# A list schedule extended through branch, output and gate/up stages, and the first two weight blocks on ACT's queue

## Chip, core and metric

The kernel runs on one core of one Trainium2 chip. The metric is the device time of one execution in microseconds (us). The engines are TensorE (PE), VectorE (DVE), ScalarE (ACT), GpSimd (POOL) and SyncE (SP); DMAs are issued from the queue of SP or of ACT.

## What is computed

A decoder block on x of 1024 tokens by 1024 channels, in float32: two mixers side by side, merged by gates, and a SwiGLU feed-forward part.

```python
xn = rms_norm(x, norm1_g)
q_sb, k_sb, v_sb, q_hg, f_hg, i_hg, g_hg, gate_sb, gate_hg = split_cols(xn @ w_in)
o_sb = stick_breaking_attention(rms(q), rms(k), v)         # 8 heads of 64
o_hg = hgrn2_mixer(q_hg, f_hg, i_hg, g_hg, lb, hg_norm_g)  # 4 heads of 128
y_sb = o_sb @ w_branch[:512]
y_hg = o_hg @ w_branch[512:]
mixed = sigmoid(gate_sb) * y_sb + sigmoid(gate_hg) * y_hg
h = x + mixed @ w_out
hn = rms_norm(h, norm2_g)
out = h + (silu(hn @ w_gate) * (hn @ w_up)) @ w_down       # 2816 hidden channels
```

## The kernel before

Channels lie on the partitions, tokens along the free axis in two halves of 512. Each float32 operand of a large product is split in two float32r parts, hi (a cast) and lo (the difference, on DVE), and a product of 128 x 128 weights with 128 x 512 data is three matmuls, hi hi, hi lo and lo hi (`mm3`, `prod`). Every such matmul is a 128x512 one. The stages follow each other:

1. S1, the stage of the mixers: x is loaded, its squares summed, xn split; 42 column blocks of `w_in` are projected (`proj`), 16 of them the gates (called G; their results go to DRAM, `sig_d`), and the heads of the two mixers run (`scores`, `values`, `hgrn`; outputs to DRAM, `o_d`). All of it is written as operations of a `Plan`: each has an engine, an estimated duration, a rank, and the buffers it needs from rings with a fixed number of slots. `Plan.issue` (L124 to L199) runs a simulated clock, and whenever an engine is free it issues the first ready operation in the order of rank and then of `way`, the longest chain of estimated durations to the end. The order found so is the instruction order of each engine (`manual_schedule`). Projections have rank -1, so PE turns to them when nothing else is ready; what remains of the G projections comes last.
2. wb, the branch products (L783 to L821): o_d is loaded and split, then for eight column blocks the gates are loaded, multiplied by the row scale `rr1` on POOL (L808), put through a sigmoid on ACT, multiplied with the products and added.
3. wo, the output projection with the residual (L834 to L890): h is stored to `h_d`, and the right operands of the next stage, `fop[1..7]`, are built from sums of its blocks (Winograd's variant of Strassen's product: seven products of half-size blocks in place of eight).
4. Gate and up (L898 to L1024): for each of 11 pairs of hidden blocks, `left` loads two weight blocks and builds seven split left operands (`a_ops`), `winograd` runs seven products of 12 matmuls for gate, and then for up. `down_sums` builds sums of the down weights for the last stage and stores them to `wd_d`; the activations and their sums go to `act_d`. The products' banks are x, y and z; y is read (`c[:, 1]`, L981; `c[:, 3]`, L986) before the next product is added into it.
5. Down (L1027 to L1102), seven products over the 11 pairs, with the residual.

Stages 2 to 5 are written in plain order and are ordered by the framework's own scheduler, which may put their instructions between those of the planned stage too. Line 182 of the profile is the one that issues every planned operation of S1. L237 and L238 are the casts and differences of `split`.

In the start, SP issues in turn the constants `vec`, x's blocks and four weight half blocks: x0, wq (first half of block q), x1, wk, x2, x3, wq (second half), x4, wk. POOL casts these weights (`split_w`). ACT's first instruction is the load of an activation table (L205). Nine dummy matmuls (L341) precede the first product.

Of the kernel before, what the change touches and what calls it, by code (L numbers as in the profile page):

```python
# [66 lines left out]
class Buf(View):  # L67
    def __init__(self, ring, make):
        super().__init__(self, lambda t: t)
        self.ring, self.make, self.tile = ring, make, None  # L70
        self.writers, self.readers, self.left, self.held = [], [], 0, False


class Plan:
# [6 lines left out]

    FROM = {"P": 0.2, "D": 2.0}
    TO = {"P": 0.35}

    def __init__(self):
        self.ops, self.caps, self.land = [], {}, {}

# [3 lines left out]
    def op(self, eng, us, calls, rank=0, after=(), part=False, holds=(), lat=None, land=None):  # L91
# [27 lines left out]
        self.ops.append((eng, us, calls, rank, deps, after, bufs, lat))  # L119
        if land:  # L120
            self.land[i] = land
        return i

    def issue(self):  # L124
# [18 lines left out]

        way = [0.0] * n
# [6 lines left out]
        early = [0.0] * n  # L151
# [6 lines left out]
        times, gone, done, t = [0.0], [], 0, 0.0  # L158
        while done < n:
# [6 lines left out]
            for e in engines:  # L166
                while free[e] <= t:
                    for i in ready[e]:
                        need = [b for b in ops[i][6] if b.ring and not b.held]
                        if early[i] <= t and all(  # L170
                                slots[b.ring] >= sum(c.ring == b.ring for c in need)
                                for b in need):
                            break
                    else:
                        break
                    ready[e].remove(i)
                    _, us, calls, rank, deps, after, bufs, lat = ops[i]
# [25 lines left out]
def hybrid_block(ctx: ExitStack, tc, xT, wi, wb, wo, wg, wu, wd, vec, outT):  # L203
    nc = tc.nc
    nc.scalar.preload_act_table_set("natural_log_exp_and_others")  # L205

# [89 lines left out]

    def hs(h):
        return slice(h * HALF, (h + 1) * HALF)
# [25 lines left out]
    xn = a_set(xst.enter_context(tc.tile_pool(name="xnp", bufs=1)))  # L324
    pre = ExitStack()
# [22 lines left out]
    st1 = ExitStack()  # L348
    tmpp = st1.enter_context(tc.tile_pool(name="tmpp", bufs=1, reuse_waits="tile"))
    stk = st1.enter_context(tc.tile_pool(name="stk", bufs=1, reuse_waits="tile"))  # L350
    att = st1.enter_context(tc.tile_pool(name="att", bufs=1, reuse_waits="tile"))
    hgp = st1.enter_context(tc.tile_pool(name="hgp", bufs=1, reuse_waits="tile"))
# [9 lines left out]
    where = {tag: (pool, cap) for pool, tags in RINGS.items() for tag, cap in tags.items()}  # L362

    def new(tag, shape=(P, HALF), dt=F32):
        pool, cap = where[tag]
        plan.ring(tag, cap)
        return Buf(tag, lambda: pool.tile(list(shape), dt, tag=tag, bufs=cap, name=tag))
# [4 lines left out]
    def A(fn, *args, n=HALF, aps=0, rank=0, ps=False, part=False, holds=(), **kw):  # L372
        us = (0.05 if ps else 0.093) + n / 1200 + 0.0935 * aps
        return plan.op("A", us, [(fn, args, kw)], rank, part=part, holds=holds)
# [23 lines left out]

    act, tt = nc.scalar.activation, nc.vector.tensor_tensor
    stt, ts = nc.vector.scalar_tensor_tensor, nc.vector.tensor_scalar  # L400

    def rstd(dst, ss, n, rank=0):
        A(act, dst, ss, AF.Ln, ps=True, aps=1, bias=eps_t, scale=1.0 / n, rank=rank)
        A(act, dst, dst, AF.Exp, scale=-0.5, rank=rank)
# [35 lines left out]
    def load(dst, src, kb):  # L440
        last_load[0] = L(dst, src, kb, rank=1, after=(last_load[0],))
# [12 lines left out]
    def take_x(h):  # L454
        ss, acc, ws, sqs = new("ms"), new("tail"), [[], []], []
        for k in range(KT):
            x = new("aa" if h == 0 else ("xf", "xq", "xi", "xg")[k // 2])
            load(x, xT[k][:, hs(h)], 256)
            if h == 0 and k in (0, 1, 3, 4):
                u, i = k % 3, k // 3  # L460
                n, v = fill[u]
                w = new("kb")
                load(w, wi[COL[n] + v][:, hs(i)], 256)
# [59 lines left out]
    def take(nm, u, h, ps):  # L523
# [17 lines left out]
        elif nm == "G":  # L541
            x = new("tmp")
            A(nc.scalar.copy, x, ps, ps=True)
            plan.op("A", 0.1, [(nc.scalar.dma_start, (sig_d[u][:, hs(h)], x), {})], lat=2.5)
# [19 lines left out]

    COL = {"q": 0, "k": 4, "v": 8, "hq": 12, "hf": 16, "hi": 20, "hg": 24, "G": 28}
# [34 lines left out]
    def values(j, last):  # L600
# [12 lines left out]
        for e in range(2):  # L613
            own, oth = slice(64 * e, 64 * e + 64), slice(64 - 64 * e, 128 - 64 * e)
            for sb in range(4):
# [29 lines left out]
                L(o_d[j][own, sb * 256:(sb + 1) * 256], ot[own], 64)  # L645
        return last

    def hgrn(hd, last):
# [5 lines left out]
        for h in range(2):  # L654
# [89 lines left out]
            L(o_d[4 + hd][:, hs(h)], o, 256)  # L744
# [3 lines left out]
    fill = [("q", 0), ("k", 0), ("v", 0), ("hf", 0), ("hq", 0), ("hi", 0)]  # L748
# [11 lines left out]
    for i, (nm, u) in enumerate(fill):  # L760
# [7 lines left out]
        elif i > 1:  # L768
            w = take_w(COL[nm] + u)
# [6 lines left out]
            if nm == "hg":  # L776
                ends = [f(u, e) for f, e in zip((scores, values, hgrn), ends)]
    with tc.manual_schedule():
        plan.issue()
    c1.close()  # L780
    st1.close()
    st2 = ExitStack()
    op_ = st2.enter_context(tc.tile_pool(name="opool", bufs=1, side="right", reuse_waits="tile"))  # L783
    mt = st2.enter_context(tc.tile_pool(name="mt", bufs=2, side="right", reuse_waits="tile"))
    oo = []
    for k in range(KT):
        t = mt.tile([P, S], F32, tag="ld", bufs=4, name="o32")
        nc.sync.dma_start(t, o_d[k])
        hi = op_.tile([P, S], F32R, name=f"oh{k}")
        lo = op_.tile([P, S], F32R, name=f"ol{k}")  # L790
        nc.scalar.copy(hi, t)
        nc.vector.tensor_tensor(lo, t, hi.bitcast(F32), op=ALU.subtract)
        oo.append((hi, lo))
    xst.close()
    mst = ExitStack()
    mx = a_set(mst.enter_context(tc.tile_pool(name="mxp", bufs=1, reuse_waits="tile")))
    wq = [get_w(wb[0])]
    for i in range(KT):
        w = wq.pop(0)
        if i + 1 < KT:  # L800
            wq.append(get_w(wb[i + 1]))
        s0 = mt.tile([P, S], F32, tag="s0", bufs=2, name="s0")
        s1 = mt.tile([P, S], F32, tag="s1", bufs=2, name="s1")
        nc.sync.dma_start(s0, sig_d[i])
        nc.sync.dma_start(s1, sig_d[KT + i])
        for s in (s0, s1):
            for h in range(2):
                nc.gpsimd.tensor_tensor(s[:, hs(h)], s[:, hs(h)], rr1[h], op=ALU.mult)  # L808
            nc.scalar.activation(s, s, AF.Sigmoid)
        for h in range(2):  # L810
            y0, y1 = pj(), pz()
            mm3(y0, w, full[:4], oo, h)
            mm3(y1, w, full[4:], oo, h)
            t0 = mt.tile([P, HALF], F32, tag="t0", name="t0")
            t1 = mt.tile([P, HALF], F32, tag="t1", name="t1")
            nc.vector.tensor_tensor(t0, y0, s0[:, hs(h)], op=ALU.mult)
            nc.vector.tensor_tensor(t1, y1, s1[:, hs(h)], op=ALU.mult)
            nc.vector.tensor_tensor(t0, t0, t1, op=ALU.add)
            nc.scalar.copy(mx[i][0][:, hs(h)], t0)
            nc.vector.tensor_tensor(mx[i][1][:, hs(h)], t0, mx[i][0][:, hs(h)].bitcast(F32),  # L820
                                    op=ALU.subtract)  # L821
    st2.close()
    rst.close()

    fst = ExitStack()
    s2p = fst.enter_context(tc.tile_pool(name="s2p", bufs=2, side="right", reuse_waits="tile"))
    fpool = fst.enter_context(tc.tile_pool(name="fpool", bufs=1, side="right", reuse_waits="tile"))
    fop = {p: [None] * 4 for p in ORDER}
    rr = [fpool.tile([P, HALF], F32, name=f"rr{h}") for h in range(2)]

    def ft(dt, name):
# [319 lines left out]
```

## Time and profile before

| | us |
|---|---|
| median of three runs (lowest, highest) | 1529.68 (1528.2, 1530.11) |
| the profiled execution's own time | 1531.17 |
| its span, first to last instruction | 1529.4 |
| PE busy | 1500.8 (98%) |
| DVE busy | 1179.9 (77%) |
| ACT busy | 799.1 (52%) |
| POOL busy | 160.5 (10%) |

The span is that of one profiled execution. Matmuls overlap each other in the array, so a busy PE counts a pipeline that holds at least one of them; a 128x512 matmul is shown with some 0.39 us and the next one starts 0.227 us later. The granted clock is given as a share of TensorE's full 2.4 GHz. A row of the windows view has start:end, the length, then for PE, PEld (PE's weight loads), DVE, ACT and POOL the busy us and (x) the number of instructions, and at the end the granted clock, the share of the DMA engines' time and GB/s.

### The profile page before, as it was taken

The numbers are of one execution on the slowest core, as the hardware profiler recorded it, in microseconds if no ns is written. First come the engines' busy times: TensorE is split into PE (matmuls) and PEld (weight loads), VectorE is DVE, ScalarE is ACT, GpSimd is POOL, SyncE is SP. The second block draws the span as 40 slices with busy tenths as digits, with TensorE's granted clock in tenths as the row PEclk, the third lists the DMA queues.
The fourth block names the chain that finished last, engine by engine and source line by source line (L and its number), as shares of the span: only waits on it lengthen the run. The fifth ranks groups of instructions, "written<-read, shape, count | busy, mean of one in ns | idle before, by whom it ended". The sixth has DMA issues, their size and how long they took to land.

```text
span 1529.4 us, 20448 instructions
## 1 busy us (share of the span) xinstructions
PE 1500.8 (98%) x7213; PEld 1241.2 (81%) x7213; DVE 1179.9 (77%) x2060; ACT 799.1 (52%) x1503; POOL 160.5 (10%) x189
## 2 busy tenths in 40 slices
PE   8999999999999999999999979999999999999999
PEld 6788888888888888888878868888888888878887
DVE  8899779987898777965557789888887777475553
ACT  7866768578858879444333352333333333254442
POOL 4210111111111110114420000000000000000000
PEclk9999999999999999999999999999999999999999
DMA  5111211111111121145434436666633333687672
GB/s 180 42 39 42 83 32 43 47 44 59 41 51 54 59 68 49 52 143 208 139 111 150 140 128 223 221 214 220 221 110 110 111 110 117 245 302 223 191 220 93
DMA packets 78407, 188.53 MB, mean 123 GB/s; under 512 B 9056, under 2 KB 11104, under 8 KB 76896
## 3 DMA queue, kind: packets, MB, share of 16 engines
q1 hardware_dynamic: 68368, 168.34, 33.7%
q10 hardware_dynamic: 9936, 18.88, 3.3%
q8 instruction: 57, 0.93, 0.3%
q14 instruction: 46, 0.38, 0.1%
HBM read 131.61 MB, written 55.57 MB: 122 GB/s over the span
## 4 chain that ended last, share of the span: by engine, by line
PE 72%; DVE 12%; DMA 6%; ACT 4%; issue 4%; POOL 2%; SPq 0%; POOLq 0%; ACTq 0%; DVEq 0%
PE pj L182 24%; PE f L919 20%; PE f L1068 12%; PE ms L182 8%; PE z L182 2%; DMA w<-wu 2%; PE pj L306 2%; PE pj L305 2%; PE pj L307 2%; DVE ol L238 2%; DMA s<-sig_d 1%; ACT aa L182 1%; DMA rb<-act_d 1%; POOL s L808 1%; DMA h_d<-xx 1%
## 5 line engine op out<-in xcount | busy, mean ns | idle before, releaser
L182 PE MATMUL pj<-ah,oh 128*128 128x512 f32 x704 | 286.6, 407 | 1.9 <-POOL oh L182 1.9
L182 PE MATMUL pj<-ah,ol 128*128 128x512 f32 x704 | 276.4, 393 | 1.1 <-DVE ol L182 1.0
L182 PE MATMUL pj<-al,oh 128*128 128x512 f32 x704 | 276.0, 392 | 0.0
L919 PE MATMUL f<-fh,oh 128*128 128x512 f32 x616 | 241.4, 392 | 11.2 <-ACT p L970 7.1
L919 PE MATMUL f<-fl,oh 128*128 128x512 f32 x616 | 240.5, 390 | 0.0
L919 PE MATMUL f<-fh,ol 128*128 128x512 f32 x616 | 240.4, 390 | 0.0
L237 ACT CAST oh<-w 128x512 fp32r<-128x512 f32 x168 | 102.5, 620 | 186.6 <-PE f L919 132.2
L182 PEld LDWEIGHTS pj<-ah,ol 128*128 128x128 f32 x704 | 132.6, 188 | 31.8 <-DVE ol L182 2.4
L182 PEld LDWEIGHTS pj<-ah,oh 128*128 128x128 f32 x704 | 133.0, 189 | 25.4 <-POOL oh L182 2.9
L182 PEld LDWEIGHTS pj<-al,oh 128*128 128x128 f32 x704 | 133.0, 189 | 22.7 <-issue 0.5
L919 PEld LDWEIGHTS f<-fh,oh 128*128 128x128 f32 x616 | 116.1, 189 | 38.4 <-ACT p L970 7.6
L238 DVE TENSOR_TENSOR ol<-w,oh 128x512 fp32r<-128x512 f32 x168 | 115.1, 690 | 35.5 <-ACT oh L237 35.2
L919 PEld LDWEIGHTS f<-fh,ol 128*128 128x128 f32 x616 | 116.1, 188 | 24.5
L919 PEld LDWEIGHTS f<-fl,oh 128*128 128x128 f32 x616 | 116.2, 189 | 23.8
L182 DVE TENSOR_TENSOR_SCAN aa<-aa,ww 128x128 f32<-128x128 f32 (+3 forms) x96 | 92.2, 975 | 33.4 <-ACT aa L182 23.9
L1068 PE MATMUL f<-bh,ah 128*128 128x512 f32 x296 | 114.9, 390 | 1.1 <-ACT acc L1094 1.1
L1068 PE MATMUL f<-bl,ah 128*128 128x512 f32 x296 | 115.4, 390 | 0.5 <-DVE bl L238 0.5
L1068 PE MATMUL f<-bh,al 128*128 128x512 f32 x296 | 115.2, 389 | 0.0
L182 POOL TENSOR_SCALAR oh<-w 128x512 fp32r<-128x512 f32 x84 | 71.1, 846 | 394.2 <-PE pj L182 355.2
L238 DVE TENSOR_TENSOR al<-ra,ah 128x512 fp32r<-128x512 f32 x73 | 50.4, 690 | 76.8 <-ACT ah L237 76.8
L237 ACT CAST ah<-ra 128x512 fp32r<-128x512 f32 x73 | 45.6, 625 | 104.0 <-PE f L1068 92.9
L182 ACT ACTIVATE aa<-aa 128x512 f32<-128x512 f32 (+3 forms) x128 | 69.1, 553 | 4.9 <-DVE aa L182 4.0
(270 smaller groups left out, 2971.2 us busy)
## 6 DMA issues: line engine op xcount, KB each, us to landing
w<-wi SPq DMA_DIRECT2D x42, 512.0 KB, 3.6
rb<-act_d SPq DMA_DIRECT2D x73, 256.0 KB, 4.4
w<-wg SPq DMA_DIRECT2D x22, 512.0 KB, 4.1
w<-wu SPq DMA_DIRECT2D x22, 512.0 KB, 3.7
w<-wd SPq DMA_DIRECT2D x22, 512.0 KB, 7.0
wd_d<-ds SPq DMA_DIRECT2D x44, 256.0 KB, 5.6
ra<-wd_d SPq DMA_DIRECT2D x44, 256.0 KB, 4.1
act_d<-c SPq DMA_DIRECT2D x10, 1024.0 KB, 3.9
```

The costliest lines, as they stand in the source:

```text
L182: fn(*[a.real() if isinstance(a, View) else a for a in args], **{k: v.real() if isinstance(v, View) else v for k, v in kw.items()})
L237: pin(nc.scalar.copy(hi, src))
L238: pin(nc.vector.tensor_tensor(lo, src, hi.bitcast(F32), op=ALU.subtract))
L305: nc.tensor.matmul(out, hi[:, ws], a[ka][0][:, hs(h)], start=first and i == 0, stop=False)
L306: nc.tensor.matmul(out, hi[:, ws], a[ka][1][:, hs(h)], start=False, stop=False)
L307: nc.tensor.matmul(out, lo[:, ws], a[ka][0][:, hs(h)], start=False, stop=last and i == n - 1)
L808: nc.gpsimd.tensor_tensor(s[:, hs(h)], s[:, hs(h)], rr1[h], op=ALU.mult)
L919: nc.tensor.matmul(out, a[i][:, ws], bl[k][j], start=start and k == 0 and i + j == 0, stop=k == 3 and i == 1, skip_group_check=True)
L1068: nc.tensor.matmul(bank[d], l[:, ws], r, start=start and i == 0, stop=p == NP - 1 and i == 2, skip_group_check=True)
```

## The change

- **The plan takes in wb, wo and gate/up.** Every operation gets a part (`s1`, `G`, `wb`, `wo`, `ffn`). Those of the later parts come after all ready ones of S1 and G on their engine (`STAGE`), and `way` counts only inside S1 and G or inside the later parts. New tile pools open when every operation of the parts named in `BEFORE` has been issued.
- **New in these stages:** the multiplications of the gates by `rr` go to DVE; temporaries of wo come from the ring `f` of 56 slots, and `t7` and `t6` overwrite `blk` tiles; `g` and `c` are four tiles of 512 columns each and are stored as four DMAs, not one; the first gate product group is ordered 1, 5, half of 2, 6, channel sums, 7, half of 2, 4, 3; PSUM banks come from the rings pj (x), ms (y) and z (z) of S1.
- **The start:** ACT issues the first halves of the blocks q and k before its table load, and casts them itself; SP's order is `vec`, x0, x1, x2, wq (second half), x3, wk (second half), x4 to x7.

Down is unchanged, but its pool of PSUM banks opens after the planned part. The core of the diff:

```diff
+    STAGE = {"s1": 0, "G": 0, "wb": 1, "wo": 1, "ffn": 1}
+    BEFORE = {0: (), 2: ("s1",), 3: ("s1", "G"), 4: ("s1", "G", "wb"), 5: ("s1", "G", "wb", "wo")}
...
-                [way[j] + delay(i, j, data) for j, data in succ[i] if ops[j][3] >= 0 or data],
-                default=0.0)
-        order = lambda i: (-ops[i][3], -way[i], i)
+                [way[j] + delay(i, j, data) for j, data in succ[i]
+                 if stage[i] == stage[j] and (ops[j][3] >= 0 or data)], default=0.0)
+        order = lambda i: (stage[i], -ops[i][3], -way[i], i)
...
-    nc.scalar.preload_act_table_set("natural_log_exp_and_others")
...
+    for n, v in fill_cols[:2]:
+        t = hgp.tile([P, HALF], F32, tag="kb", bufs=4, name="kb")
+        nc.scalar.dma_start(t, wi[COL[n] + v][:, :HALF])
+        first_w.append(t)
+    nc.scalar.preload_act_table_set("natural_log_exp_and_others")
...
+            for u in range(2):
+                w = Buf("kb", lambda u=u: first_w[u])
+                hi, lo = new("oh", dt=F32R), new("ol", dt=F32R)
+                plan.at[A(nc.scalar.copy, hi, w, rank=3)] = 2.4 + 0.6 * u
+                V(tt, lo, w, hi.bitcast(F32), op=ALU.subtract, rank=2)
+                ws[u].append((hi, lo))
...
-            if h == 0 and k in (0, 1, 3, 4):
-                u, i = k % 3, k // 3
+            if h == 0 and k in (2, 3):
+                u = k - 2
...
+    mx = []
+    for i in range(KT):
+        w = get_w(wb[i])
...
+            for h in range(2):
+                V(tt, t[:, hs(h)], t[:, hs(h)], rr[h], op=ALU.mult)
+            A(act, t, t, AF.Sigmoid, n=S + (0 if i or ss else TABLE))
...
+                    t7, t6 = blk[0, 1], blk[0, 0]
+                    V(tt, t7, y, t7, op=ALU.subtract)
+                    V(tt, t6, t7, t6, op=ALU.add)
...
+    def winograd(a, ring, first=False):
+
+        c = [new(ring) for _ in range(4)]
+        x, y, z, p1 = new("pj"), new("ms"), new("z"), new("p1")
+        prod(x, a, 1, True)
+        A(nc.scalar.copy, p1, x, ps=True)
+        if first:
+            prod(z, a, 5, True)
+            prod(x, a, 2, False, (0, 1))
+            prod(y, a, 6, True)
+            channel_sums()
+            V(tt, c[1], y, p1, op=ALU.add)
+            prod(y, a, 7, False)
+            prod(x, a, 2, False, (2, 3))
...
+    for p in range(NP):
+        au = left(wu, p, "wA")
+        x, g = winograd(ag, "g", p == 0)
...
+        for b, t in enumerate((*c, n7, n6, n5, n4)):
+            dst = actd[p][:, b * HALF:(b + 1) * HALF]
+            store_a(dst, t) if p == NP - 1 else L(dst, t, 256, part=True)
+
     with tc.manual_schedule():
         plan.issue()
-    c1.close()
-    st1.close()
```

## Rows read from the trace of the kernel before

**Rows 1.** windows by stage: start:end, then length, busy us of engines, clock, DMA

```profile
21.21:702.10 680.89, 674.65 (x3620) 564.29 (x3620) 566.27 (x1074) 487.74 (x984) 113.24 (x141) 1.00 0.19 61
702.10:790.80 88.70, 87.29 (x385) 71.95 (x384) 51.90 (x73) 32.42 (x45) 38.22 (x28) 1.00 0.36 123
790.80:877.86 87.06, 87.06 (x385) 72.07 (x384) 62.59 (x105) 32.05 (x56) 0.00 (x0) 1.00 0.43 138
877.86:1313.23 435.37, 424.19 (x1854) 348.49 (x1852) 361.58 (x582) 144.67 (x239) 0.00 (x0) 0.99 0.47 160
```

**Rows 2.** windows over single gate/up pairs of 168 matmuls

```profile
936.89:976.13 39.24, 38.42 (x169) 31.46 (x169) 34.67 (x57) 11.93 (x20) 0.00 (x0) 1.00 0.62 215
...
1053.95:1092.73 38.78, 38.38 (x168) 31.45 (x168) 34.57 (x57) 12.00 (x21) 0.00 (x0) 1.00 0.64 217
1092.73:1130.83 38.10, 38.09 (x168) 31.52 (x169) 32.24 (x52) 12.55 (x22) 0.00 (x0) 1.00 0.51 164
```

**Rows 3.** waits of PE, whole kernel: total us, times, longest

```profile
PE f L919 <- ACT p L970: 7.1, 1, 7.1
PE f L919 <- DVE g L981: 3.0, 5, 0.8
...
PE z L305 <- DVE t L817: 1.4, 1, 1.4
```

**Rows 4.** timeline of PE from wo into gate: start, us, instruction, idle before

```profile
885.12 0.39 PE L919 MATMUL f<-fh,ol 128*128 128x512 f32 x1
892.64 0.79 PE L919 MATMUL f<-fh,oh 128*128 128x512 f32 x1 [7.14 <-ACT p L970]
...
897.08 0.42 PE L919 MATMUL f<-fl,oh 128*128 128x512 f32 x1
...
898.24 1.09 PE L932 MATMUL f<-parts,ones_r 128*128 128x512 f32 x4
...
905.34 0.50 PE L919 MATMUL f<-fh,oh 128*128 128x512 f32 x1 [0.99 <-DVE g L986]
```

**Rows 5.** timelines of ACT and DVE, same stretch

```profile
892.01 0.58 ACT L970 COPY p<-f 128x512 f32<-128x512 f32 x1
...
885.43 0.69 DVE L884 TENSOR_TENSOR t<-yy 128x512 f32<-128x512 f32 x1 [2.89 <-DMA h_d<-xx]
```

**Rows 6.** chain that ended last, and waits of SP's queue, 905 to 1095

```profile
957.49 5.71 DMA w<-wu
...
SPq L958 <- DVE ds L945: 79.6, 16, 10.8
```

**Rows 7.** groups by line: count, busy us and mean ns, idle before

```profile
L808 POOL TENSOR_TENSOR s<-s,rr 128x512 f32<-128x512 f32 x32 | 43.3, 1380 | 59.5 <-DMA s<-sig_d 59.5
```

**Rows 8.** timeline of PE in the start

```profile
5.68 0.74 PE L182 MATMUL pj<-ah,oh 128*128 128x512 f32 x1
...
9.17 0.50 PE L182 MATMUL pj<-ah,oh 128*128 128x512 f32 x1 [1.85 <-POOL oh L182]
...
20.94 0.39 PE L182 MATMUL pj<-ah,ol 128*128 128x512 f32 x1
```

**Rows 9.** timelines of SP, ACT and POOL in the start

```profile
1.24 0.41 SPq L182 DMA_DIRECT2D aa<-xT  x1
...
0.80 1.28 ACT L205 ACT_TABLE_LOAD   x1 [0.80 <-PEq L1133]
...
8.05 1.07 POOL L182 TENSOR_SCALAR oh<-kb 128x512 fp32r<-128x512 f32 x1 [2.42 <-DMA kb<-wi]
```

**Rows 10.** windows of the start

```profile
1.24:4.27 3.03, 2.83 (x7) 2.25 (x8) 1.78 (x15) 1.14 (x3) 2.48 (x4) 1.00 0.67 180
4.27:7.13 2.86, 2.73 (x7) 1.22 (x5) 1.82 (x3) 1.24 (x2) 0.62 (x1) 1.00 0.86 216
...
9.17:17.00 7.83, 7.54 (x26) 5.68 (x26) 7.83 (x12) 7.83 (x15) 4.24 (x8) 0.78 1.05 393
```

**Rows 11.** windows of 25 us, second one

```profile
25.00:50.00 25.00, 22.70 (x94) 17.07 (x93) 23.28 (x38) 16.47 (x28) 15.09 (x21) 1.00 0.15 43
```

More of the change, by code (lines that the diff above doesn't have):

```diff
@@ L169, in issue @@
                         need = [b for b in ops[i][6] if b.ring and not b.held]
-                        if early[i] <= t and all(
+                        if early[i] <= t and not any(
+                                left[p] for p in self.BEFORE[phase[i]]) and all(
                                 slots[b.ring] >= sum(c.ring == b.ring for c in need)
@@ L369, in fixed, with new, make, A @@
+    def new(ring, shape=(P, HALF), dt=F32):
+        pool, cap, tag, phase = where[ring]
+        plan.ring(ring, cap)
+        def make():
+            open_pools(phase)
+            return (pools[pool] if phase else pool).tile(list(shape), dt, tag=tag, bufs=cap, name=tag)
+        return Buf(ring, make, phase)
     def fixed(tile):
         return Buf(None, lambda: tile)
-    def A(fn, *args, n=HALF, aps=0, rank=0, ps=False, part=False, holds=(), **kw):
+    def A(fn, *args, n=HALF, aps=0, rank=0, ps=False, part=False, holds=(), after=(), **kw):
@@ L776, in hybrid_block, with full_split, get_w @@
             if nm == "hg":
+                plan.part = "s1"
                 ends = [f(u, e) for f, e in zip((scores, values, hgrn), ends)]
+    def full_split(src, rings=("oh", "ol"), rank=0):
+        hi, lo = new(rings[0], dt=F32R), new(rings[1], dt=F32R)
+        A(nc.scalar.copy, hi, src, rank=rank)
+        V(tt, lo, src, hi.bitcast(F32), op=ALU.subtract, rank=rank)
+        return hi, lo
+    def get_w(src):
+        t = new("w", (P, 1024))
+        load(t, src, 512, rank=0)
+        return [full_split(t[:, 512 * i:512 * i + 512]) for i in range(2)]
@@ new lines, in hybrid_block, with products @@
+    TABLE = 1536
+    plan.part = "wb"
+    turn = last_fill[0]
+    oo = []
+    for k in range(KT):
+        t = new("ld", (P, S))
+        L(t, od[k], 512)
+        hi, lo = new("oo", (P, S), F32R), new("oo", (P, S), F32R)
+        A(nc.scalar.copy, hi, t, n=S)
+        V(tt, lo, t, hi.bitcast(F32), op=ALU.subtract, n=S)
+        oo.append((hi, lo))
+    def products(out, w, a, ks, h, k0=0, last=True):
+        nonlocal turn
+        for n, k in enumerate(ks):
+            hi, lo = w[(k0 + n) // 4]
+            ws = slice((k0 + n) % 4 * P, ((k0 + n) % 4 + 1) * P)
+            turn = M(1536, [(out, hi[:, ws], a[k][0][:, hs(h)], n == 0, False),
+                            (out, hi[:, ws], a[k][1][:, hs(h)], False, False),
+                            (out, lo[:, ws], a[k][0][:, hs(h)], False, last and n == len(ks) - 1)],
+                     after=(turn,))
@@ new lines, in hybrid_block, with left @@
+    last_wu, last_wd = [None], [None]
+    def left(src, p, ring):
+        A_ = "A" if ring == "wA" else ""
+        sp = lambda t: full_split(t, ("oh" + A_, "ol" + A_))
+        ta, tb = new(ring, (P, 1024)), new(ring, (P, 1024))
+        for t, r in ((ta, src[p]), (tb, src[p + NP])):
+            if A_:
+                last_wu[0] = L(t, r, 512, after=(last_wu[0],))
+            else:
+                load(t, r, 512, rank=0)
+        a11, a12, a21, a22 = ta[:, :512], ta[:, 512:], tb[:, :512], tb[:, 512:]
+        s2 = new("s2")
+        ops = {1: sp(a11)}
+        V(tt, a21, a11, a21, op=ALU.subtract)
+        V(tt, s2, a22, a21, op=ALU.subtract)
+        ops[6] = sp(s2)
+        V(tt, a11, s2, a11, op=ALU.add)
+        ops[5] = sp(a11)
+        ops[7] = sp(a21)
+        ops[2] = sp(a12)
+        ops[4] = sp(a22)
+        V(tt, a12, a12, s2, op=ALU.subtract)
+        ops[3] = sp(a12)
+        return ops
```

447 lines of the change are left out of this document (206 added, 241 removed).

## The prediction

> **What bounds the kernel now.** I read the profile stage by stage first: one row of the windows view for each stage [rows 1]. TensorE (PE) is busy in 674.65 of the 680.89 us of the first stage (the hand-written list schedule, S1 below), 87.29 of 88.70 in the branch stage (wb), all 87.06 of the output projection (wo), and 424.19 of 435.37 in gate and up. So PE is the bound throughout, and only what PE doesn't do can be won: idle time, time at the lower clock, and late starts inside "busy". For the floor of a stage I take its own best stretch. Wo, with the same 384 matmuls as wb, took 87.06 us, 0.227 us each: wb loses 88.70 - 87.06 = 1.64. One gate/up pair of 168 matmuls ran without a gap in 38.10 us [rows 2]; eleven make 419.1, and the four channel-sum matmuls [rows 4] at 0.227 each 0.9. Gate/up loses 435.37 - 420.0 = 15.3 us. That is the largest loss with one address, and the list schedule is extended over exactly that stage.
>
> Next, who ended PE's waits [rows 3]: one wait of 7.1 us in gate/up for ACT's copy `p1` (L970), five of at most 0.8 for DVE's L981, one of 1.4 in wb (bank z, L305).
>
> **Gate/up, part by part.** Its first product group ends near 885.35; PE starts again at 892.64 [rows 4]: 7.3 us. When it starts, ten matmuls need 897.08 - 892.64 = 4.44 us instead of 2.27: the granted clock was at its lower level, 1.2 GHz, after that idle stretch, another 2.2 us. Why was ACT's copy so late? It ran at 892.01, behind casts of the weight splits and of `fh`, which wait for DVE; DVE itself stood 2.89 us at 885.43 because `t7` (L884) takes a slot whose old content, `xx`, was still being stored to h_d [rows 5]. The change removes both: `t7` becomes `blk[0, 1]` in place, `xx` comes from the ring of 56, and `p1` goes onto ACT by its rank on the path, not behind splits that aren't due. All of 7.3 + 2.2 can go. What takes its place is DVE: after the last wo matmul it owes some 10 instructions of the last block, 6 of gate's weight splits, 2 channel sums, 5 evacuations and 8 of up's splits before the 20 us of the first winograd are over: 31 at 0.62 us (32.24 us for 52, [rows 2]) = 19 us. It fits with nothing to spare, so I leave 2.5 us of stalls here. Bounds: 0, and the 9.5 us of before.
>
> The pairs from 936.89 on: four stretches last 39.24 to 38.78 rather than 38.10 [rows 2], with waits of up to 0.8 [rows 3]. In each the chain runs through a load of `w<-wu`, issued only at 957.49 and landing 5.71 us later [rows 6]; SP had waited 79.6 us in this window on L958, a store of `ds` queued ahead of it on SP's one queue. In the plan, down_sums and its stores have a short way to the end and the loads of wu go when their slots are free. The four stretches lose some 3.5 us, the wait at 905.34 [rows 4] 1.0 (half of which I keep, since the new order still puts only 6 matmuls between the last read of y and its overwrite) and what is left of the 15.3, 1.3, lies before 936.89: 5.8 in all, of which I leave 1.0. Gate/up then: 15.3 - 2.5 - 1.0 = **11.8 us won**; bounds 3.5 (below, rival 3) and 15.3.
>
> **wb.** 32 multiplications by rr move from POOL (1380 ns) to DVE (0.62 for one of its instructions, as above) [rows 7]: +19.8 us on DVE, 51.90 + 19.8 = 72 of 88.70. DVE has that room; were it gone, PE would wait for the banks pj and z. The result comes sooner by two POOL latencies, and the last z bank with it. I take 1.3 of the 1.64; bounds -1 and 1.64. The loads of o_d and the branch weights stay covered by the tail of G projections, pure PE work, as before. Wo has nothing to win.
>
> **The start.** PE's first real matmul is at 5.68 and the last of the first 48 (two blocks, eight k, three products) starts at 20.94 [rows 8]: 15.5 us with its own for 48 x 0.227 = 10.9 us of work. The cause is `wk`'s first block: SP issues x0, wq, x1, wk in turn from 1.24, and `wk` lands so late that POOL splits it only at 8.05, and PE waits until 9.17 [rows 8, 9]. Afterwards both blocks go from ACT's queue, whose first instruction is at 0.80 [rows 9]; its table load (1.28) follows them and is done at about 3.0, before ACT has data. x0 and x1 go from SP in parallel. The four blocks, 1 MB, are in by about 7.1 at the rates of before (180 GB/s to 4.27, then 216 [rows 10]), so the six matmuls of k = 0 go at about 6.2 rather than at 5.68 to 10.9, and from x1 (7.1, a cast of 0.6 to 0.7 and a difference of the like: about 8.6) PE needs 1.36 us for each k, against 0.66 us for 256 KB at 393 GB/s [rows 10]. The first half ends at 8.6 + 7 x 1.36 = 18.1, or 2 later at the lower clock that the gap may leave: 1.1 to 3.1 earlier than before. ACT pays two casts (0.5 each), POOL loses them. Then some is given back: at 25 to 50 us DVE is busy 23.28 of 25 and PE only 22.70 [rows 11], so PE's lead runs into evacuations. I take **1.7 us**; bounds -0.5 and 4.6.
>
> The Trainium skill ("DMA: Bandwidth & Descriptors", section "Issuing engines are not separate DMA queues") speaks against this part: transfers issued from several engines run on the same 16 DMA engines and interleave, so only issue time is saved. The rows agree in part: between 4.27 and 7.13 the engines were 86% busy at 216 GB/s [rows 10], so there was hardly a free engine. By the rule alone the start wins the 0.44 us between 0.80 and 1.24 [rows 9]; by my sum 1.7, because the order of the blocks changes too.
>
> **S1 after the start.** Costs and ranks are the same, but a list schedule that starts with other times puts other instructions first. PE idles 680.89 - 674.65 = 6.2 us here; I take 0, bounds -4 (more idle) and +3.
>
> **Down.** It is scheduled outside the plan; its first operands are loaded ahead into wpool. The eight stores of the last pair now sit on ACT (five before), three of them early. The new pool of banks lies on old ones, of which the last z is read after the last product. I take 0; bounds -2 and +0.5. The end after the last matmul stays.
>
> **Sum.** 11.8 + 1.3 + 1.7 = 14.8 us. The profiled execution took 1531.17 (span 1529.40, 1.77 around it), which gives 1516.4; the median of the runs is 1.49 below that execution, so 1529.68 - 14.8 = **1514.9 us**, a gain of 1.0%.
>
> **Rivals.**
> 1. *One pipe.* x0 shares the DMA engines with the two weight blocks and lands late; the start wins no more than the 0.44 us by which ACT can issue before SP's x0. This is the Trainium skill's rule above. Speaks for it: 86% busy at 216 GB/s [rows 10]. Against: `wk`'s split by 8.05 was fourth in line. Time 1514.9 + 1.3 = 1516.2.
> 2. *S1 is reshuffled to the worse.* 4 us more idle PE and the start's gain lost: 1514.9 + 5.7 = 1520.6. For: DVE at 93% of 25 to 50 us [rows 11], G work is finite filler. Against: 674.65 of 680.89 busy shows how much filler there is.
> 3. *DVE takes the wait over.* In the plan's ranks evacuations that feed only stores (c times g, the last adds of x and z) stand behind the splits of every later product. DVE has 38.10 - 32.24 = 5.9 us to spare for a pair [rows 2]. If each of eleven pairs stalls 0.9 us, the stage needs 420.0 + 2 + 9.9 = 431.9, 3.5 won: 1523.2. Against: the four split slots hold the splits back, so DVE has gaps for the rest.
> 4. *Slower: SP's order.* SP now has twelve stores a pair in one fixed order with six loads. The plan reckons 3.5 us for a 512 KB load; 5.71 was seen [rows 6]. If a store that waits for DVE stands ahead of a gate load in every pair, with 2 us of idle PE, 22 us are lost: with the 4.8 won on the pairs gone too, 1514.9 + 4.8 + 22 = 1541.7. It decides from (14.8 - 4.8)/11 = 0.9 us a pair. For: L981 shows just such a wait. Against: slots come free two thirds of a pair before their content is due.
> 5. *S1 gains too,* 3 us of its 6.2, and the whole 15.3: 1508.4.
>
> **How the numbers follow.** Chances: my forecast (1510 to 1519) 0.45, rival 1 0.18, rival 2 0.12, rival 3 0.09, rival 4 0.09, rival 5 0.07. The range 1508 to 1527 leaves out rival 4 and the ends of the others. A measurement of this kernel tells 0.2%, about 3 us, from nothing. Forecast and rivals 1 and 5 are faster (0.70); of rival 2 and 3 (0.21) two thirds are, the rest within 0.2%: faster 0.84, same 0.07, slower 0.09.
>
> **What would show it.** In the changed profile: no wait of PE above 1 us and no stretch of lower clock near the first gate product; gate/up about 423.6 us from its first to its last product; pairs at 38.1 to 38.3 from the third on; wb at 87.1 to 87.4 with no POOL multiplications; first 48 matmuls done by 18 to 20. I'm wrong if pairs stay at 39 or more, if a new wait stands between wo and gate, or if S1 idles above 10 us.

## The result, and the profile after

The changed kernel takes 1531.65 us (median, 1528.2 to 1534.13); the kernel before, beside it, 1529.11 (1526.87 to 1531.88). The ratio is 1.0018, with an interval of 1.0011 to 1.0024: slower by 0.2%, where 1.0% faster was forecast. The profiled execution of the changed kernel is its fastest (1528.2, span 1526.5), that of before one of its longer ones (1531.17, span 1529.4), so the two traces differ the other way round; what a typical execution loses besides comes from a second profile of the changed kernel (e4_again, below).

Windows by stage of the changed kernel: S1 after the start, wb, wo, gate/up, down. The columns are those of [rows 1].

```profile
17.50:700.14 682.64, 675.09 (x3617) 563.10 (x3616) 575.74 (x1082) 492.93 (x989) 100.47 (x132) 1.00 0.19 62
700.14:787.20 87.06, 87.06 (x386) 72.10 (x385) 66.07 (x106) 35.71 (x48) 0.00 (x0) 1.00 0.39 129
787.20:874.20 87.00, 87.00 (x385) 72.08 (x384) 61.56 (x102) 34.55 (x58) 0.00 (x0) 1.00 0.41 137
874.20:1308.00 433.80, 426.23 (x1854) 348.91 (x1853) 357.99 (x578) 140.99 (x236) 0.00 (x0) 0.99 0.48 160
1308.00:1522.60 214.60, 211.28 (x925) 172.72 (x923) 120.00 (x189) 86.14 (x152) 0.00 (x0) 1.00 0.69 223
```

S1 ends 1.96 us earlier than in [rows 1], wb is 1.64 shorter, and gate/up only 1.57: 433.80 against 435.37, where 423.6 was forecast. Down is 2.1 longer (1313.23 to 1525.70 before, 212.47). The join that the forecast spoke of is mended, as the timeline of PE there shows beside [rows 4]: the 7.14 us wait has become 0.20.

```profile
885.04 0.73 PE L194 MATMUL ms<-f,oh 128*128 128x512 f32 x2 [0.20 <-DVE g L194]
```

So the loss is new, and it lies later. Windows of about one pair each, of the changed kernel (columns as above), beside [rows 2]:

```profile
874.20:912.70 38.50, 38.30 (x168) 31.11 (x167) 36.20 (x60) 22.15 (x35) 0.00 (x0) 1.00 0.54 178
912.70:951.20 38.50, 34.68 (x143) 27.21 (x142) 33.09 (x54) 11.54 (x20) 0.00 (x0) 0.96 0.75 241
951.20:989.60 38.40, 37.90 (x167) 30.78 (x166) 36.09 (x60) 11.23 (x20) 0.00 (x0) 1.00 0.80 263
989.60:1028.00 38.40, 35.35 (x152) 28.30 (x151) 34.13 (x56) 10.96 (x19) 0.00 (x0) 0.99 0.81 267
...
1066.00:1104.00 38.00, 38.00 (x170) 31.45 (x169) 30.51 (x50) 11.82 (x21) 0.00 (x0) 1.00 0.34 111
```

The first pair is nearly full. In the second and fourth PE gets through 143 and 152 matmuls instead of 168; from 1066 on nothing is lost. The DMA column goes with it: 0.75 to 0.81 of the engines, then 0.34. (In before's four pairs from 936.89 on it stood at 0.62 to 0.64.) The waits of PE, then of DVE, then of SP's queue in this stretch, of the changed kernel (the first over all of gate/up, the others to 1060), beside [rows 3, 6]:

```profile
PE z L194 <- DVE ol L194: 3.9, 4, 1.9
PE ms L194 <- DVE g L194: 2.3, 3, 1.3
PE z L194 <- ACT oh L194: 1.4, 2, 1.2
```

```profile
DVE ds L194 <- DMA w<-wd: 6.6, 5, 1.9
DVE w L194 <- DMA w<-wu: 3.2, 3, 1.4
```

```profile
SPq L194 <- DVE ds L194: 56.1, 36, 10.7
```

PE waits 3.9 + 2.3 + 1.4 = 7.6 us, 6.2 of it for DVE; DVE waits most for the loads of `wd`, which only `down_sums` needs, and whose result nobody reads before the down stage. One such wait, followed through the timeline of DVE and then of PE:

```profile
926.50 0.69 DVE L194 TENSOR_TENSOR ds<-w 128x512 f32<-128x512 f32 x1 [1.89 <-DMA w<-wd]
...
927.72 0.68 DVE L194 TENSOR_TENSOR ol<-w,oh 128x512 fp32r<-128x512 f32 x1
928.44 0.69 DVE L194 TENSOR_TENSOR ds<-w,ds 128x512 f32<-128x512 f32 x1
929.05 0.68 DVE L194 TENSOR_TENSOR g<-ms,p 128x512 f32<-128x512 f32 x1
```

```profile
929.79 0.73 PE L194 MATMUL ms<-f,oh 128*128 128x512 f32 x2 [0.73 <-DVE g L194]
```

DVE stands 1.89 us for a load of wd; the split `ol` and the evacuation `g` are behind it in DVE's fixed order, and PE waits for `g`. The Trainium skill ("PSUM — Partial Sum Buffer", section "Engine vs sequencer instructions") says that the queues of ScalarE and VectorE are strictly first in, first out; this trace agrees, with the 1.89 us by which everything behind that `ds` moved. Not every wait of PE has such a load right before it: ahead of the longest, 1.88 at 943.75, DVE has been at work without a gap since 937.5, behind its earlier waits. The DMA view of this stretch and a view of the tile give the rest: all 22 loads of wd are issued by 1029 and take 5.7 us each (median), and the sums run from 886.1 to 1044.5 (below, the first of a pair's four).

```profile
w<-wd SPq DMA_DIRECT2D x22, 512.0 KB, 5.7
w<-wu SPq DMA_DIRECT2D x8, 512.0 KB, 5.1
```

```profile
L194 DVE TENSOR_TENSOR ds<-w x11: 679/686/692, 886.1 to 1031.9; 128x512 f32<-128x512 f32 x11
```

Gate/up then adds up: 433.80 - 420.0 (the floor of the prediction) = 13.8, of which 433.80 - 426.23 = 7.57 is idle, and 6.2 is PE "busy" with more than 420 us. Some 3.4 of these are two stretches at a lower clock, right behind waits of PE that end at 943.75 and 1026.41:

```profile
944.00:949.00 5.00, 5.00 (x16) 3.98 (x16) 5.00 (x9) 1.76 (x3) 0.00 (x0) 0.66 0.45 138
1024.00:1034.00 10.00, 8.32 (x28) 6.40 (x29) 8.00 (x13) 3.89 (x7) 0.00 (x0) 0.83 0.65 197
```

That is 5 x 0.34 + 10 x 0.17 = 3.4; the other 2.8 were not followed up. The waits go with a loss of almost twice their length.

In the start, PE's first real matmul comes at 5.99 and the stream is hardly broken. Windows of PE alone, of before and then of the changed kernel:

```profile
0.00:60.00 60.00, 53.10 (x208) 0.97 0.40 132
60.00:120.00 60.00, 58.63 (x312) 1.00 0.15 47
120.00:400.00 280.00, 279.40 (x1520) 1.00 0.16 47
```

```profile
0.00:60.00 60.00, 56.51 (x230) 1.00 0.38 132
60.00:120.00 60.00, 58.31 (x304) 1.00 0.14 46
120.00:400.00 280.00, 276.75 (x1514) 1.00 0.16 48
```

After 60 us PE is 56.51 - 53.10 = 3.4 us ahead, and some 60 x 0.03 = 1.8 more by the clock; between 60 and 400 it gives 0.3 + 2.65 back in waits that the order of before didn't have. The clock's part is not the same in every execution: over these 60 us the four profiles with the old start show 0.94 to 0.97, the ten with the new one 1.00, except e9_acc's with 0.97. The multiplications by rr are on DVE now, 684 ns each, beside [rows 7]:

```profile
L194 DVE TENSOR_TENSOR s<-s,rr x32: 681/684/694, 689.0 to 770.7; 128x512 f32<-128x512 f32 x32
```

### The profile page after: what moved, and what is told of

Same layout as the page of the kernel before. It is cut to its first block, busy times and chain, and to the rows that moved or that the text cites. A ratio compares the mean times of both kernels' runs of the same rounds, so it can differ in the third digit from the quotient of the medians.

```text
span 1526.5 us, 20498 instructions
## 1 busy us (share of the span) xinstructions
PE 1502.3 (98%) x7213; PEld 1240.0 (81%) x7213; DVE 1196.1 (78%) x2092; ACT 804.3 (53%) x1505; POOL 109.2 (7%) x155
## 4 chain that ended last, share of the span: by engine, by line
PE 77%; DVE 12%; DMA 5%; ACT 3%; issue 3%; POOL 1%; SPq 0%; DVEq 0%; ACTq 0%; POOLq 0%
PE pj L194 37%; PE ms L194 17%; PE f L1150 12%; PE z L194 11%; DVE ol L194 2%; DVE aa L194 1%; DMA w<-wu 1%; DMA hb<-h_d 1%; DMA rb<-act_d 1%; DVE g L194 1%; ACT aa L194 1%; DVE kb L194 1%; DVE tail L194 1%; DMA w<-wd 1%; DMA w<-wg 1%
## 5 line engine op out<-in xcount | busy, mean ns | idle before, releaser
L194 DVE TENSOR_TENSOR ol<-w,oh 128x512 fp32r<-128x512 f32 x248 | 170.0, 686 | 42.5 <-ACT oh L194 35.6
L194 PE MATMUL ms<-f,oh 128*128 128x512 f32 x528 | 163.8, 392 | 2.3 <-DVE g L194 2.3
L194 PEld LDWEIGHTS ms<-f,oh 128*128 128x128 f32 x528 | 99.6, 189 | 24.5 <-DVE g L194 3.5
L194 DVE TENSOR_TENSOR_SCAN aa<-aa,ww 128x512 f32<-128x512 f32 (+3 forms) x96 | 94.2, 996 | 25.3 <-ACT aa L194 14.6
L194 PE MATMUL z<-f,oh 128*128 128x512 f32 x352 | 110.3, 395 | 1.4 <-ACT oh L194 1.4
L194 PE MATMUL pj<-f,oh 128*128 128x512 f32 x352 | 108.4, 389 | 0.0
L194 PE MATMUL ms<-f,ol 128*128 128x512 f32 x264 | 103.0, 390 | 0.0
L194 POOL TENSOR_SCALAR oh<-w 128x512 fp32r<-128x512 f32 x84 | 67.2, 800 | 437.6 <-PE pj L194 367.5
L194 PEld LDWEIGHTS z<-f,oh 128*128 128x128 f32 x352 | 66.6, 190 | 16.2 <-ACT oh L194 2.5
L194 PE MATMUL pj<-mx,oh 128*128 128x512 f32 x256 | 78.9, 389 | 0.0
```

The costliest lines, as they stand in the source:

```text
L194: fn(*[a.real() if isinstance(a, View) else a for a in args], **{k: v.real() if isinstance(v, View) else v for k, v in kw.items()})
```

## The experiments

Times of different runs are compared by their ratio to the kernel before on the same chip.

**e1_pace**: the changed kernel, but the loads for a pair's `down_sums` wait in the plan for that pair's last gate matmul.

```diff
-            last_wd[0] = L(t, r, 512, after=(last_wd[0],))
+            last_wd[0] = L(t, r, 512, after=(last_wd[0], turn))
```

> The changed kernel, but the two loads of the down weights of a pair may start only after that pair's last gate matmul (one more dependency in the plan). Theory A, sums for the down stage are drawn forward: in the changed kernel all 22 loads and 44 stores of the down sums ran between 874 and 1045 us, DVE waited 6.6 us for those loads inside its fixed order, and every wait of PE in gate/up lies in that time; paced, gate/up takes 420 to 425 us instead of 433.8, with no wait above 0.5 us, and the kernel 1520 to 1524. Theory B, DVE is simply behind after the output projection and needs five pairs to catch up whatever else it does: the waits stay where they are, gate/up 431 to 436, the kernel 1529 to 1533.

1518.07 us, ratio 0.9937 (0.9925 to 0.995). Stage windows, gate/up and down:

```profile
874.90:1296.51 421.61, 421.14 (x1853) 347.32 (x1852) 359.40 (x578) 142.00 (x236) 0.00 (x0) 1.00 0.48 164
1296.51:1511.60 215.09, 211.72 (x925) 174.07 (x923) 120.18 (x189) 86.19 (x152) 0.00 (x0) 0.99 0.68 223
```

Gate/up is 12.2 us shorter with the same number of DVE instructions (578), no wait of PE above 0.20 in it, and a busy time of 421.14 in place of 426.23. What DVE has to do is no obstacle (rival 3 falls); where the sums stand in its order is. Down is as long as in the changed kernel: 215.09.

**e2_start**: before with the new start alone (two blocks on ACT's queue and cast by ACT, x's blocks first on SP). The core of the edit:

```diff
...
+    for n, v in (("q", 0), ("k", 0)):
+        t = hgp.tile([P, HALF], F32, tag="kb", bufs=4, name="kb")
+        nc.scalar.dma_start(t, wi[COL[n] + v][:, :HALF])
...
```

> The kernel before with the new start alone (two weight blocks from ACT's queue and cast by ACT, x0, x1, x2 first on SP); the branch, output and gate/up stages are left to the framework's scheduler. Theory A, what PE wins in the start is kept to the end of the first stage but for what a new order costs: 48 matmuls done by about 17.5 us, the branch stage begins 1.5 to 3.5 us earlier than 702.1, the kernel 1526 to 1528. Theory B, the first stage gives all of it back: branch stage at 701.5 to 703, the kernel 1528.5 to 1530.5.

1529.4 us, ratio 1.0003 (0.9993 to 1.0012): nothing that can be measured. In its profile the last G product begins 1.3 us earlier than before's (700.57 against 701.83), and the wait between wo and gate is still there, 6.36 us long.

**e3_list**: the changed kernel with the start of before. The core of the edit:

```diff
...
-        t = hgp.tile([P, HALF], F32, tag="kb", bufs=4, name="kb")
-        nc.scalar.dma_start(t, wi[COL[n] + v][:, :HALF])
...
-                plan.at[A(nc.scalar.copy, hi, w, rank=3)] = 2.4 + 0.6 * u
...
+            if h == 0 and k in (0, 1, 3, 4):
+                u, i = k % 3, k // 3
...
```

> The changed kernel with the old start (all four weight half blocks from SP, cast by POOL). If the two parts of the change add, this is the changed kernel plus the 2 us that its first stage ended earlier: 1533 to 1535, gate/up 432 to 437 us. If the first stage's new order had cost what the start won, it is the changed kernel or better: 1529 to 1531.

1532.05 us, ratio 1.0027 (1.0016 to 1.0037). So the longer list alone gives the loss. Waits of PE in its gate/up:

```profile
PE z L194 <- DVE ol L194: 7.0, 5, 2.0
```

**e4_again**: the changed kernel once more, for the profile of a typical execution.

> The changed kernel once more. Its first profile was its fastest run of twenty (1528.2 against a median of 1531.65). If the 3 us between are in gate/up, where loads collide, this profile shows gate/up at 435 to 438 us instead of 433.8 and the first stage, branch and output stages within 0.5 us of before's profile of it; if they are in the first or the down stage, those differ by 2 us or more.

1531.26 us, ratio 1.0017 (1.0008 to 1.0025); the profile is of an execution of 1531.98. Its gate/up takes 434.69 and its down 217.4, against 433.80 and 214.60 in the first profile. Windows of its down stage around one wait of 3.13 us, which PE has at 1344.03 for ACT's copy `acc`:

```profile
1309.19:1344.00 34.81, 31.06 (x133) 24.36 (x131) 18.20 (x28) 13.68 (x25) 0.00 (x0) 0.99 1.02 365
1344.00:1354.00 10.00, 9.97 (x32) 8.02 (x33) 9.04 (x16) 6.30 (x12) 0.00 (x0) 0.70 0.96 329
```

Behind the wait the granted clock is 0.70 over 10 us, 32 matmuls instead of some 45. In the first profile the same wait (2.88) has no such stretch. That is most of the 3.8 us between the two executions.

**e5_hb** and **e6_sp** take up this wait, both on top of e1_pace, where it is 3.06. In e5_hb the 16 `hb` loads that ACT issues in the first down product are spread over two products:

```diff
-            if o == 1 and p >= 3:
-                for k, h in HB[2 * p - 6:2 * p - 4]:
-                    nc.scalar.dma_start(hb[k][:, hs(h)], h_d[k][:, hs(h)])
+            if (o == 1 and p >= 3) or (o == 2 and p < 8):
+                k, h = HB[p - 3 if o == 1 else 8 + p]
+                nc.scalar.dma_start(hb[k][:, hs(h)], h_d[k][:, hs(h)])
```

> The paced changed kernel (e1_pace) with the sixteen hb loads of the down stage spread: one per p instead of two in product 1 from p = 3 on, and the other eight in product 2. Theory D (the transfers of product 1 are the bound there: its DMA share was 1.03 to 1.04 at 1310:1345, and ACT's casts and with them the acc copy come late): the PE wait for the acc copy, 3.06 in e1_pace, falls to 1 or less, the stage from 215 to about 212.5, and with no lower clock behind the wait the time is about 1515 to 1516. Rival S (ACT stands behind the eight stores of the last pair that are on its queue): the wait stays near 3 and the time within 1 of e1_pace's 1518.1. Rival L (more casts stand ahead of the acc copy in ACT's fixed order): stays near 3 too, unless the order of the casts moves.

1521.67 us, ratio 0.9955 (0.9942 to 0.9967), whose interval overlaps e1_pace's. The wait became longer, on PE, more than any expectation had:

```profile
1337.27 0.79 PE L1150 MATMUL f<-bh,ah 128*128 128x512 f32 x1 [10.32 <-ACT acc L1176]
```

In ACT's timeline the copies at 1336.64 stand behind casts of the second product, two of which start late, after 3.54 and 3.50 us:

```profile
1331.36 0.62 ACT L247 CAST ah<-ra 128x512 fp32r<-128x512 f32 x1 [3.54 <-DMA hb<-h_d]
...
1336.12 0.62 ACT L247 CAST ah<-ra 128x512 fp32r<-128x512 f32 x1 [3.50 <-DMA rb<-act_d]
1336.64 1.06 ACT L1176 COPY acc<-f 128x512 f32<-128x512 f32 x2
```

The chain that ended last shows what the first of them stood behind: ACT's issue of an `hb` load at 1330.93, which itself waited for an earlier `hb` load to land.

```profile
1325.20 5.71 DMA hb<-h_d
...
1330.93 0.33 ACTq L1169
```

For the second the profile names a load of `rb`, and two more issues of `hb` (1334.32 and 1335.67) stand just ahead of it. So the edit relieved the transfers (DMA share 0.92 from 1316 to 1345, against 1.04 from 1316 to 1340 in e1_pace), but put issues of `hb` ahead of the copy too. It gives the theory of the transfers no support, and can't refute it alone; e9_acc, below, decides.

e6_sp puts the last pair's stores on SP's queue:

```diff
-            store_a(dst, t) if p == NP - 1 else L(dst, t, 256, part=True)
+            L(dst, t, 256, part=True)
```

> The paced changed kernel with the last pair's eight act_d stores on SP's queue instead of ACT's. Rival S: ACT reaches its casts earlier, the acc wait of 3.06 falls to 1 or less and the time to about 1515 to 1516. Theory D: the wait stays at about 3; the stores now stand ahead of the down stage's first loads on SP, so the first down product may begin some 1 to 3 later than in e1_pace: 1518 to 1521.

1521.62 us, ratio 0.995 (0.9938 to 0.9962). PE still waits 2.2 for `acc`, against 3.06, and 4.8 more for a cast of operands, whose loads now stand behind the stores on SP. The stores on ACT aren't what holds the copy back for most of its wait.

**e7_before_pace**: the kernel before with pacing alone. The two wd loads of a pair stand on SP behind the last store of the pair before it.

```diff
-            nc.sync.dma_start(ta, wd[p])
-            nc.sync.dma_start(tb, wd[p + NP])
+            with (tc.issue_after(stored[0]) if p else ExitStack()):
+                nc.sync.dma_start(ta, wd[p])
+                nc.sync.dma_start(tb, wd[p + NP])
...
```

> The kernel before with one edit alone: the two wd loads of pair p stand on SP behind the last act_d store of pair p-1, so that the sums can't run ahead of their pair. If the crowding by the early sums is what the first pairs lose before as well as after (5.8 in the pairs before), gate and up take 435.4 - 4.8 = about 430.6, with the 7.1 wait ahead of the first gate product still there, and the time falls by 4 to 6, to about 1523.5. Rival: the first pairs' waits of before have another cause (the hand-written order, splits behind evacuations), and the time stays within 1 of before's.

1525.11 us, ratio 0.9975 (0.9966 to 0.9984): 3.9 us faster, with the two wd loads of a pair held back and no new list. Waits of PE in its gate/up, where lines stand one further down from L949 on; beside [rows 3, 4] the five for L981 are gone, and the one for L986 (here L987) is as it was:

```profile
PE f L919 <- ACT p L971: 6.1, 1, 6.1
PE f L919 <- DVE g L987: 1.0, 1, 1.0
```

So the early sums were the trouble of before's first pairs too. They cost something else there: DVE has no wait for wd among its listed waits of before, but 5.0 us for `wu` from 897 to 1095, which are 1.4 in e7_before_pace. That fits what the prediction made of these pairs, loads of wu queued behind the stores of the sums.

**e8_at**: e1_pace whose planner takes ACT's two first blocks for ready at 3.4 and 5.5 instead of 2.4 and 3.0.

```diff
-                plan.at[A(nc.scalar.copy, hi, w, rank=3)] = 2.4 + 0.6 * u
+                plan.at[A(nc.scalar.copy, hi, w, rank=3)] = 3.4 + 2.1 * u
```

> The paced changed kernel whose planner takes the two blocks on ACT's queue for ready at 3.4 and 5.5 instead of 2.4 and 3.0 (ACT's casts of them began at 3.93 and 6.03). Only the plan's order changes. If the 1.8 to 2 that S1 gives back comes from an order planned on a start that the chip doesn't keep, the last G product ends nearer 698.5 than 700.6 and the time falls by 1 to 2 against e1_pace's 1518.1. Rival: S1 is set by waits that any such order has; its end moves by no more than 0.7 either way and so does the time.

1520.9 us, ratio 0.9945 (0.9932 to 0.9957), which overlaps e1_pace's. The last G product begins at 701.43, not 2 earlier than e1_pace's 700.62, and e11_pace_again, the same kernel as e1_pace, has 701.42. A truer start of the plan doesn't give S1's loss back. The profile shows more: e8_at has done 208 matmuls after 60 us, no more than before, e11_pace_again 225, and both end S1 at the same time. So a lead of PE at 60 us doesn't by itself reach the end of S1.

**e9_acc**: e1_pace with ACT's casts for the second down product, from its second p on, put behind the copies.

```diff
-            ops = operands(o, p)
+            with (tc.issue_after(copied[0]) if o == 2 and p >= 1 else ExitStack()):
+                ops = operands(o, p)
...
-                nc.scalar.copy(acc1[d], bank[d])
+                copied = [nc.scalar.copy(acc1[d], bank[d]).ins]
```

> The paced changed kernel (e1_pace) with ACT's casts for the second down product, from its p = 1 on, put behind the acc copies, so that two casts instead of seven stand between ACT's last hb loads and the first acc copy. Rival L (the casts ahead in ACT's fixed order): 5 x 0.52 = 2.6 of the 3.06 wait go, it falls to 0.5 or so, the half clock behind it (0.83 at 1330:1340 in e1_pace, some 1.7) goes too, p = 1 may wait 0.4 for its casts; the time falls by 2 to 4 against e1_pace, to about 1514 to 1516. Theory D (transfers): it no longer stands after the spread loads made the wait 10.32; by it the wait stays at 3 and the time within 0.5 of e1_pace.

1516.13 us, ratio 0.9917 (0.9904 to 0.9931), against 0.9941 (0.9928 to 0.9953) for e1_pace in the same run: the best version here, 12.7 us faster than before. Its gate/up and its down stage:

```profile
875.65:1297.10 421.45, 420.90 (x1854) 347.40 (x1852) 359.83 (x578) 141.78 (x236) 0.00 (x0) 1.00 0.48 164
1297.10:1510.20 213.10, 210.96 (x925) 172.87 (x923) 120.00 (x189) 86.10 (x152) 0.00 (x0) 1.00 0.68 225
```

ACT's timeline of e9_acc, the casts and the copies behind them:

```profile
1327.34 0.62 ACT L247 CAST ah<-ra 128x512 fp32r<-128x512 f32 x1 [1.63 <-PE f L1150]
1327.87 0.62 ACT L247 CAST bh<-rb 128x512 fp32r<-128x512 f32 x1
1328.39 2.04 ACT L1177 COPY acc<-f 128x512 f32<-128x512 f32 x4
```

Two casts at 0.52 each stand ahead of the copies, where e1_pace has seven and before three (waits of 3.06 and 1.07: the four casts between them are 2.08). The first and the last line of this stretch of ACT in e1_pace, with five more casts and no gap between them and the copy:

```profile
1326.22 0.62 ACT L247 CAST ah<-ra 128x512 fp32r<-128x512 f32 x1 [2.44 <-PE f L1150]
...
1329.87 0.57 ACT L1176 COPY acc<-f 128x512 f32<-128x512 f32 x1
```

The longest waits of PE in e9_acc's down stage:

```profile
PE f L1150 <- DVE bl L248: 1.8, 3, 1.2
```

The wait for `acc` is gone; 1.2 of it has moved to the splits of the next operands.

**e10_land**: the changed kernel, not paced; only the planner's landing time of the two loads is raised. The plan adds it to 512/350 = 1.46 us of transfer, so it now reckons 7.2 for a load of wd instead of 3.5, somewhat more than the 5.7 seen.

```diff
-            last_wd[0] = L(t, r, 512, after=(last_wd[0],))
+            last_wd[0] = L(t, r, 512, after=(last_wd[0],), land=5.7)
...
-                last_wu[0] = L(t, r, 512, after=(last_wu[0],))
+                last_wu[0] = L(t, r, 512, after=(last_wu[0],), land=5.1)
```

> The changed kernel as it was timed, not paced, whose planner reckons a wd load to land after 5.7 and a wu load after 5.1 instead of 2.0 (the durations that the traces show). If the cheap landing is why the sums run ahead and DVE's order stands behind them, the plan alone spaces them and gate and up fall from 434 to 421.6 to 426: 1519 to 1524. Rival: the sums run ahead because nothing orders them behind their pair, whatever a load costs; 22 wd loads still fall before about 1060, the waits of gate and up stay near 9 to 10 in sum, and the time stays at 1529 to 1532.

1519.99 us, ratio 0.9941 (0.9928 to 0.9953), as much as pacing gives in the same run; gate/up takes 422.64. But the plan hardly spaces the sums: they run from 887.8, as early as in the changed kernel, and the engines of the DMA are nearly as full (0.70 to 0.76 against 0.75 to 0.81). The wd loads take 5.4 us. A view of the tile and pair windows, of e10_land:

```profile
L194 DVE TENSOR_TENSOR ds<-w x11: 682/685/690, 887.8 to 1054.2; 128x512 f32<-128x512 f32 x11
```

```profile
912.70:951.20 38.50, 38.50 (x172) 31.87 (x171) 36.16 (x60) 11.67 (x20) 0.00 (x0) 1.00 0.76 251
951.20:989.60 38.40, 38.34 (x169) 31.44 (x168) 35.42 (x59) 11.87 (x20) 0.00 (x0) 1.00 0.70 221
989.60:1028.00 38.40, 37.55 (x165) 30.45 (x164) 35.00 (x58) 11.79 (x20) 0.00 (x0) 1.00 0.76 241
```

What is gone is DVE's wait: none for wd is left among its waits to 1060. That separates two things that e1_pace changes together. A DMA share of 0.76 costs PE 0 in one of these pairs and 0.85 in another; a DVE that stands in line for one of these loads costs more. The edit raises the price of wu too, and DVE's wait for wu is gone with the other; but e1_pace keeps 2.6 us of that wait to 1060, with no wait of PE above 0.20, so it is the wait for wd that counts. My expectation had them as one and put the gain down to the spacing, which hardly happened.

**e11_pace_again** and **e12_old_start** were measured beside the two.

> e1_pace once more, beside the two above and the one below on the same chip: 0.9937 of before's time, 0.9925 to 0.995, about 1518 to 1520.

1519.84 us, ratio 0.9941 (0.9928 to 0.9953).

e12_old_start is e9_acc with the start of before; its edit is that of e3_list.

> e9_acc with the start of the kernel before (all weight blocks by SP and split by POOL, x's blocks between them). The difference to e9_acc is what the new start is worth once the rest is in order: 1.3 to 1.9 by the end of the last G product in the profiles (702.07 against 700.16 to 700.62), so about 1.5 above e9_acc. Rival: as in e2_start, whose median was within 0.4 of before's, nothing of it is left: within 0.5.

1518.1 us, ratio 0.9929 (0.9915 to 0.9942), 2.0 above e9_acc, with overlapping intervals. Its last G product begins at 701.71, only 0.36 later than e9_acc's 701.35; of the rest, 1.15 is a wait for `acc` that this order still has. Over all profiles the last G product begins at 699.92 to 701.59 with the new start (ten profiles) and at 701.71 to 702.07 with the old one (four), so the start's own worth is between 0.1 and 2.2; by the times of e2_start it can't be told from nothing.

## Why the prediction was wrong, step by step

**The step that failed** is in the paragraph on the pairs: "In the plan, down_sums and its stores have a short way to the end and the loads of wu go when their slots are free", from which I left 1.0 us of the pairs' 5.8; measured against e9_acc, where the sums are held back, the loss was 433.80 - 421.45 = 12.4 us. A short way to the end puts an operation last among those that are ready, and nothing more: whenever the plan sees a free engine and no better candidate, it takes it. So the sums filled every gap that DVE had in the plan, all eleven pairs' within the first four and a half. The gaps were planned with a load that takes 3.5 us (1.46 and 2.0 to land); on the chip it took 5.7, and DVE stood in its fixed order in front of the splits and evacuations. I had the price in hand: rival 4 says that the plan reckons 3.5 and that 5.71 was seen. But I charged it to SP's stores, and not to DVE, which is in order too; SP waits 63.0 us for `ds` to 1060 in e10_land (56.1 in the changed kernel) with hardly a loss on PE. e1_pace (later loads) and e10_land (a higher price) each take DVE's wait for wd away, and the time follows: both -0.6% against before. e7_before_pace (later loads in the old kernel) gives -0.25%, with the waits for L981 gone.

**The join** was right: 7.14 became 0.20, and the first pair lost 0.2 of 38.5 us where I left 2.5 for DVE's backlog. With the sums in place e9_acc's gate/up takes 421.45, between the floor of 420.0 and the 423.6 forecast: 13.9 won for my 11.8.

**wb** won 1.64 for 1.3 taken, at the floor of wo (87.06).

**The start** was under-sized and **S1** over-sized, and the errors cancel for the most part. The start brings a lead of 3.4 + 1.8 us at 60 us, above the 1.7 taken and its upper bound of 4.6. S1 then gave back about 3 by 400 us (term 0, bound -4). At its end 0.1 to 2.2 are left (1.96 in the first profile, 1.3 in e2_start, 0.36 between e9_acc and e12_old_start). What sets the waits of S1 was tried once (e8_at) and stays open. The Trainium skill's rule ("DMA: Bandwidth & Descriptors", section "Issuing engines are not separate DMA queues") was taken in the prediction to give 0.44; the lead at 60 us differs from it, the end of S1 is too scattered to tell. The new order in which the blocks land, the casts on ACT and the clock changed together, and no run separates them.

**Down** was taken at 0, with a bound of -2: it lost 2.1 in the first profile and about 4.9 in the second. I thought of the operands and of the stores, not of ACT's order: the cast count ahead of `acc` went from three to seven, 3.06 - 1.07 = 2.0 us between those two profiles, and with it came, in some executions, a stretch at a lower clock. The size varies: with the same seven casts the wait is 2.13 in e11_pace_again, where PE has stood 1.4 us for casts shortly before, and 3.21 in e8_at, so the order cost 1.1 to 2.1 more than that of before. e9_acc bears the count out, and e6_sp shows that the stores make up little of it. Why the framework's scheduler put more casts ahead, with the code of that stage unchanged, was not followed up.

**The rivals.** None was it. Rival 3 had the engine (DVE takes the wait over) without the cause; rival 4 had the cause's price at the wrong queue, and took its loss as one of every pair, 0.9 us for each of eleven, where the 12.4 us were lost in the first four and a half. My signs for being wrong were the pairs, the join and S1; the pairs from the fifth on are at 38.0, and the four before them showed it.

**The sum, once the two orders are mended.** In the profile of e9_acc (span 1514.1): start and S1 0.5, wb and wo 1.7, gate/up 13.9, down -0.6, end -0.2, together 15.3 less than before's span of 1529.4. Before's profile is one of its longer executions and e9_acc's one of its two shortest; by the medians it is 12.7. My 14.8 was about what the change can give, not what this plan of it gave.

## What to carry to other kernels

A list schedule is a promise to in-order engines: a load that is priced at 3.5 us and takes 5.7 stalls whatever engine has its consumer in line, so price loads by the landing time that a trace of the kernel shows, or hold back the work that nobody needs soon. Here the loads of wd took 5.4 to 7.0 us (medians) whether they were crowded or paced (6.4 in e1_pace, at a DMA share of 0.48), so traffic alone isn't why 3.5 was too little. A short way to the end doesn't hold work back; a dependence does. Before costing a moved operation at nothing, count what stands ahead of the next critical instruction on its engine: here four more casts of 0.52 us made 1 to 2 us of PE's idle time.

## What was not expected of the hardware

The same wait of about 3 us for `acc` left PE's granted clock at 1.00 (2.88, the changed kernel), 0.70 (3.13, e4_again), 0.83 (3.06, e1_pace) and 0.83 (3.21, e8_at) over the 10 us behind it. The first two are executions of one program, and at 0.70 it costs it some 3 us. Whether that is why the times of the changed kernel spread over 1528 to 1534 isn't shown: e9_acc's four lie within 1.1 us, but e12_old_start's five, with a wait of 1.15, spread over 3.1.

And 0.76 of the DMA engines in use at 251 GB/s left PE's pair at 38.5 of 38.5 us busy in e10_land: in that pair the traffic took nothing from the matmuls.
